# Two output tiles of a linear unit, product by product in turn instead of one after the other

## The chip, the core and the metric

The kernel runs on one core of a Trainium2 chip. Its engines work side by side, each through its own list of instructions in order: TensorE (PE, matrix products; its weight loads, PEld, run beside the products), VectorE (DVE), ScalarE (ACT), GpSimd (POOL) and the DMA queues. TensorE writes its results to PSUM, eight banks of 512 float32 per partition; DVE and ACT read them from there into SBUF. The metric is the device time of one execution in microseconds.

## The reference

Two layers over 256 latent tokens (`x`) and 256 context tokens (`ctx`), model width 1024. Per layer:

```
m = silu(c) @ w_mod + b_mod                                  # shifts, scales, gates
xn = rmsnorm(x, norm1) * (1 + m[1]) + m[0]                   # the context likewise, with c_ctx
u = xn @ w_in                                                # queries, keys, values, gates, z of three mixers
ya = blockwise_attend(...); yb = window_attend(...); yc = gdn_out(gated_delta(...), z)
y = (sig(ga)*(ya @ w_pa) + sig(gb)*(yb @ w_pb) + sig(gc)*(yc @ w_pc)) @ w_out
x = x + m[2] * y
x = x + m[5] * conv_ffn(rmsnorm(x, norm2) * (1 + m[4]) + m[3])   # silu(a) * b, width 2816, depthwise conv
```

The output is the final RMSNorm of the latent tokens. The second layer's context stream is needed only as keys, values and state, so most of that layer's linears have 256 columns and the first layer's have 512.

## The kernel before

Activations stand feature-major: a tile is 128 features by 512 tokens (context first, then latent). Every float32 value that a linear multiplies is cut in two parts of the type float32r, a high part H and the rest L, and a product is replaced by three: H·XH, H·XL, L·XH (`mm3`, L202 to L206; the three lines L204, L205, L206 are the three products, and most rows of the profile on TensorE stand under them).

`linear` (L278) goes through the weight matrix in units of 256 output features, that is two tiles of 128 features, each with a PSUM bank of its own. The weights of a unit come in loads of 4 feature blocks (512 KB): `load_split` (L186) transfers them (`raw`, three buffers), ACT rounds them to H (`wh`, L194, three buffers) and DVE or POOL forms L (`wl`, L184, four buffers). One load holds the columns of both tiles. For each load `products` (L303) issues all twelve products of the first tile (4 blocks of 3), then all twelve of the second. After its last load a tile is evicted by `evac`, at raised priority. So the first tile of a unit is finished twelve products before the second.

```
for i in range(nt):
    due = g
    for k in range(g):
        ...
        self.mm3(pss[i][:, cs[i]], H[:, k, cc], L[:, k, cc], XH[kg + k][:, cs[i]], XL[kg + k][:, cs[i]], ...)
```

PSUM is shared out by two tags: `mm` has three banks, `g` has five (L161). Outside the merge, the output projection and the feed-forward all units take their two banks from `mm`; in those three stages (`self.wide`) units take them from `mm` and `g` by turns. Everything else on TensorE (attention, the delta rule, transposes, norms) uses `g`.

The work around the linears is written as generators: a chain (delta rule or attention) yields the time that it leaves free, and `fill` (L219) emits queued linears for that long. A linear yields after every two feature blocks of one tile (`ly` = 2, six products). The library's scheduler then fixes the order of each engine's list from the order of emission, from priorities and from its own estimates; on the chip each engine goes through its list strictly in order.

What evicts a unit: the delta rule's projections one ACT and two DVE operations (L664, L667, L669), the gates a sigmoid on ACT (L1374), plain projections a copy on ACT or DVE by turns (L540, L538), the merge a DVE product (L1538, L1540), the residuals one DVE operation (L1560), the feed-forward one ACT and two DVE operations (L1600, L1603, L1605). `gdn_misc`, `proj_sq`, `linear_first` and the latent attention's values call `mm3` or its lines directly.

Of the kernel before, what the change touches and what calls it, by code (L numbers as in the profile page):

```python
# [11 lines left out]
PSUM = bass.MemoryType.PSUM  # L12
# [4 lines left out]
T = 512  # L17
S = 256
# [11 lines left out]
def make_consts():  # L30
    """Constants that depend on shapes alone: identities, masks, rotation tables."""
# [73 lines left out]
class _Tok:  # L105
    """[:, streams, tile] of a [p, 512] view: the chunks (0, 3) or (1, 2) of each stream."""
# [9 lines left out]
class Lat(float):  # L116
    """Yielded: what comes next waits for other engines, for about so many microseconds."""


class _Pri:  # L120
    """An engine whose instructions are scheduled as if they came `off` instructions earlier."""
# [13 lines left out]
class Kernel:  # L135
# [41 lines left out]
    def split_L(self, out, x, h):  # L177
        """out = x - h, exact: h is x rounded to 12 significant bits."""
        self.lacc += self.lpool
        e = self.nc.vector  # L180
        if self.lacc >= 1.0:
            self.lacc -= 1.0
            e = self.nc.gpsimd
        e.tensor_tensor(out=out, in0=x, in1=h.bitcast(F32), op=ALU.subtract)  # L184

    def load_split(self, srcs, shape):  # L186
        """Weights to SBUF (pieces: (view of the tile, source)), split exactly in two float32r parts."""
# [31 lines left out]
    def fill(self, us, burst=0.0):  # L219
        """Emit queued independent work worth about us microseconds of the tensor engine."""  # L220
# [17 lines left out]
    def bg_steps(self):  # L238
        """Steps of a later modulation while the second stream's norm is on its way."""
# [7 lines left out]
    def gate_step(self):  # L247
        """A step of the gates that are computed ahead; its time."""
# [11 lines left out]
    def ahead(self, credit=None):  # L260
        """Let the gates fill the wait of what comes next."""
# [5 lines left out]
    def gsync(self):  # L267
        """Complete the gates' unit in progress."""
        while self.gates is not None and self.gate_n[0] > self.gate_n[1]:
            self.gate_step()  # L270

    def finish(self, *gens):
        """Emit what is left of the queued gens."""
# [5 lines left out]
    def linear(self, w, k0, nk, c0, ncol, X, evac, cols=None, kgrp=4, split=None, hook=None, gate=False):  # L279
        """Feature-major product: evac(i, psum, cols) gets rows i*128.. of w[k0*128:, c0:c0+ncol].T @ X  # L280
        (c0 a tuple: the first columns of two tiles).
        The unit of columns `split` takes one stream after the other; the generator hook() advances within the
        second (or within the first, if the unit is the first)."""
        XH, XL = X
        for u0 in range(0, ncol, 256):
# [17 lines left out]
            def products(kg, wt, cs):  # L303
                """The products of one load, and each tile's evacuation after its last; yields per tile."""
                g, H, L = wt
                for i in range(nt):
                    due = g
                    for k in range(g):
                        cc = slice(i * 128, i * 128 + 128)
                        self.mm3(pss[i][:, cs[i]], H[:, k, cc], L[:, k, cc], XH[kg + k][:, cs[i]], XL[kg + k][:, cs[i]],  # L310
                                 kg + k == 0, kg + k == nk - 1)
                        if hk:
# [3 lines left out]
                        elif k % self.P["ly"] == self.P["ly"] - 1 and k < g - 1:  # L316
                            yield (cs[i].stop - cs[i].start) * self.P["ly"] * 3 / 2400
                            due -= self.P["ly"]
                    if kg + g == nk:
                        with self.tc.high_priority(self.P["hpe"]):  # L320
                            evac(u0 // 128 + i, pss[i], cs[i])
                    yield (cs[i].stop - cs[i].start) * due * 3 / 2400
# [18 lines left out]
    def rstd(self, out, ss, scale, shape, post=1.0):  # L341
        """out = post / sqrt(ss * scale + eps); for more than a few values a first guess from the bits, then Newton steps
        to float32's accuracy."""
# [15 lines left out]
    def stat(self, x, cs, first, e=None, alloc=True, last=False):  # L359
        """Add the squares of x to the running sums of columns cs; the last ones are added by stat_rstd's products."""  # L360
# [13 lines left out]
    def stat_rstd(self, cs, dim, wait=1.5):  # L374
        """Broadcast (in PSUM) 1/rms of the columns from the running sums; yields between its products."""
# [18 lines left out]
    def norm_mod(self, x, A, B, XH, XL, s, r=None, ks=range(KD)):  # L394
        """XH + XL = x * rstd * A + B for the columns of stream s."""
# [56 lines left out]
    def modulation_first(self):  # L452
        """Parts 0 and 1 of layer 0's modulation, the first half of the features before the second."""
# [26 lines left out]
    def first_norm(self, hf):  # L480
        """The features of one half, normed and modulated, of layer 0's input."""
# [7 lines left out]
    def linear_first(self, w, c0, X, evac):  # L489
        """As linear, 512 columns: the products of the first half of the features, while the modulation of the second is on its way."""  # L490
# [23 lines left out]
    def load_x(self):  # L514
# [3 lines left out]
        # x, ctx: token-major loads, transposed on PE  # L518
# [23 lines left out]
    def load_vectors(self, l):  # L542
        """The layer's vectors, one row per 128 values, transposed; yields between loads and transposes (of those first needed, and the rest)."""
# [21 lines left out]
    def load_conv(self, l):  # L565
        """The feed-forward's convolution weights, transposed."""
# [15 lines left out]
    def modulation(self, l, cg, room="raw"):  # L582
        """Parts 2cg and 2cg+1 of the modulation of layer l."""
# [25 lines left out]
    def mod_A(self, l, j, ks=slice(0, KD)):  # L609
        """A = norm * (1 + scale); j = 0 for norm1, 1 for norm2."""  # L610
# [1113 lines left out]
```

## Time and profile before

| | |
|---|---|
| three timed runs | 1824.82, 1826.38, 1837.09 us; median 1826.38 |
| span of the profiled execution (first to last instruction) | 1830.3 us; its own device time is not listed apart |
| TensorE busy | 1712.1 us (94%), 12343 instructions |
| weight loads busy | 1364.8 us, 12343 instructions |
| DVE, ACT, POOL busy | 1083.0, 773.8, 569.8 us |
| mean granted TensorE clock | 0.966 of full speed |

One execution was profiled. Each instruction has a start and a duration; products are pipelined, so the durations of neighbours overlap and the pace is read from their starts. "Idle before" with an arrow names what ended an engine's wait. The windows view gives busy time per engine in stretches of the span, with the mean granted clock of TensorE (1.00 is 2.4 GHz, 0.50 is 1.2 GHz).

### The profile page before, as it was taken

How to read it: one execution, taken by the hardware profiler on the slowest of the kernel's cores; microseconds unless marked ns; L12 is line 12 of the kernel's file. 1: busy time of each engine (PE TensorE's matmuls, PEld its weight loads, DVE VectorE, ACT ScalarE, POOL GpSimd, SP SyncE). 2: the span in 40 equal slices, each digit the busy share in tenths (PEclk: the TensorE clock that was granted, in tenths of full speed). 3: DMA queues.
4: the chain of work that ended last, by engine and by line, in shares of the span. 5: the costliest groups of instructions: out<-in, count | busy, mean ns of one | idle time of the engine just before them, and what ended most of it. 6: DMA issues, size and time to landing. Idle time of an engine off the chain costs nothing. (4 is left out here: it accounts for less than half of the span.)

```text
span 1830.3 us, 30777 instructions
## 1 busy us (share of the span) xinstructions
PE 1712.1 (94%) x12343; PEld 1364.8 (75%) x12343; DVE 1083.0 (59%) x2041; ACT 773.8 (42%) x1375; POOL 569.8 (31%) x405
## 2 busy tenths in 40 slices
PE   8899978999999999999999999889888899989997
PEld 4667764776557888558888888768777767989997
DVE  3778384464865443435425544688687776667574
ACT  3474311233756233324324333455513376555453
POOL 2152621332210423012212222152833331534242
PEclk9899989999999999999999999989988899989999
DMA  8423316233134543753332344323433223745653
GB/s 306 130 69 104 94 47 208 71 75 110 52 118 147 187 130 112 265 172 115 95 101 92 93 154 150 93 76 105 110 82 69 59 81 102 227 136 173 187 172 129
DMA packets 216941, 228.70 MB, mean 125 GB/s; under 512 B 51228, under 2 KB 195422, under 8 KB 215646
## 3 DMA queue, kind: packets, MB, share of 16 engines
q1 hardware_dynamic: 211582, 220.11, 39.6%
q10 hardware_dynamic: 4928, 6.56, 1.0%
q8 instruction: 97, 1.59, 0.4%
q14 instruction: 46, 0.38, 0.1%
q0 software_dynamic: 288, 0.06, 0.0%
HBM read 213.85 MB, written 11.80 MB: 123 GB/s over the span
## 5 line engine op out<-in xcount | busy, mean ns | idle before, releaser
L184 POOL TENSOR_TENSOR wl<-raw,wh 128x1024 fp32r<-128x1024 f32 (+3 forms) x124 | 285.2, 2301 | 700.5 <-ACT wh L194 643.1
L194 ACT CAST wh<-raw 128x1024 fp32r<-128x1024 f32 (+2 forms) x294 | 297.9, 1017 | 433.2 <-PE mm L205 195.9
L204 PE MATMUL mm<-xnh,wh 128*128 128x512 f32 (+2 forms) x1072 | 386.1, 361 | 7.5 <-DVE b L669 5.2
L206 PE MATMUL mm<-xnh,wl 128*128 128x512 f32 (+2 forms) x1072 | 379.7, 355 | 10.9 <-POOL wl L184 7.1
L205 PE MATMUL mm<-xnl,wh 128*128 128x512 f32 (+2 forms) x1072 | 380.1, 355 | 2.8 <-DVE xnl L411 2.8
L184 DVE TENSOR_TENSOR wl<-raw,wh 128x1024 fp32r<-128x1024 f32 (+1 forms) x170 | 211.1, 1243 | 197.4 <-ACT wh L194 184.6
L206 PEld LDWEIGHTS mm<-xnh,wl 128*128 128x128 f32 (+1 forms) x1072 | 209.2, 195 | 45.6 <-POOL wl L184 10.0
L204 PEld LDWEIGHTS mm<-xnh,wh 128*128 128x128 f32 (+1 forms) x1072 | 209.9, 196 | 44.4 <-issue 10.3
L205 PEld LDWEIGHTS mm<-xnl,wh 128*128 128x128 f32 (+1 forms) x1072 | 209.9, 196 | 34.8 <-issue 6.2
L204 PE MATMUL g<-xnh,wh 128*128 128x256 f32 (+1 forms) x496 | 167.1, 339 | 1.4 <-ACT xnh L410 1.4
L205 PE MATMUL g<-xnl,wh 128*128 128x256 f32 (+1 forms) x496 | 166.5, 337 | 1.8 <-DVE xnl L411 1.8
L206 PE MATMUL g<-xnh,wl 128*128 128x256 f32 (+1 forms) x496 | 166.4, 337 | 0.0
L205 PE MATMUL mm<-s,wh 128*128 128x256 f32 (+1 forms) x458 | 150.2, 329 | 2.4 <-DVE s L1204 1.3
L204 PE MATMUL mm<-s,wh 128*128 128x256 f32 (+1 forms) x458 | 151.1, 331 | 1.0 <-DVE s L538 0.5
L206 PE MATMUL mm<-s,wl 128*128 128x256 f32 (+1 forms) x458 | 150.2, 330 | 0.0
L204 PEld LDWEIGHTS g<-xnh,wh 128*128 128x128 f32 x496 | 94.3, 191 | 18.8 <-issue 6.7
L1621 POOL TENSOR_TENSOR b<-b,b 128x512 f32<-128x512 f32 (+1 forms) x44 | 53.8, 1223 | 163.5 <-DVE b L1605 156.4
L205 PEld LDWEIGHTS g<-xnl,wh 128*128 128x128 f32 x496 | 94.5, 191 | 13.4 <-DVE xnl L411 2.5
L206 PEld LDWEIGHTS g<-xnh,wl 128*128 128x128 f32 x496 | 94.5, 191 | 12.2 <-issue 2.5
L205 PE MATMUL g<-s,wh 128*128 128x512 f32 (+1 forms) x304 | 102.4, 337 | 0.9 <-DVE s L200 0.9
L204 PE MATMUL g<-s,wh 128*128 128x512 f32 (+1 forms) x304 | 102.8, 338 | 0.4 <-ACT s L199 0.4
L206 PE MATMUL g<-s,wl 128*128 128x512 f32 (+1 forms) x304 | 102.4, 337 | 0.0
(289 smaller groups left out, 2926.1 us busy)
## 6 DMA issues: line engine op xcount, KB each, us to landing
raw<-in_w_in_dram SPq DMA_DIRECT2D x92, 512.0 KB
raw<-in_ffn_up_dram SPq DMA_DIRECT2D x80, 512.0 KB
s<-in_w_mod_dram SPq DMA_DIRECT2D x64, 512.0 KB
raw<-in_w_mod_dram SPq DMA_DIRECT2D x32, 512.0 KB
raw<-in_ffn_down_dram SPq DMA_DIRECT2D x32, 512.0 KB
raw<-in_w_out_dram SPq DMA_DIRECT2D x16, 512.0 KB
raw<-in_ffn_down_dram SPq DMA_DIRECT2D x16, 384.0 KB
spill<-s SPq DMA_DIRECT2D x4, 1024.0 KB
```

The lines of the kernel that those rows point to most:

```text
L184: e.tensor_tensor(out=out, in0=x, in1=h.bitcast(F32), op=ALU.subtract)
L194: nc.scalar.copy(H, raw)
L204: mm(ps, lhsT=wH, rhs=xH, start=start, stop=False)
L205: mm(ps, lhsT=wH, rhs=xL, start=False, stop=False)
L206: mm(ps, lhsT=wL, rhs=xH, start=False, stop=stop)
L1621: nc.gpsimd.tensor_tensor(out=y[:, cs], in0=y[:, cs], in1=av[t][:, cs], op=ALU.mult)
```

## The change

Within `products` the loop over the two tiles moves from the outside to the inside. For each feature block the three products are issued kind by kind, and within a kind first for one tile and then for the other: H·XH into bank 0, H·XH into bank 1, H·XL into bank 0, H·XL into bank 1, L·XH into bank 0, L·XH into bank 1. The moving operand of two neighbours is the same, the bank and the weight block change with every product. Number, size and operands of the products stay as they are, and so does their order within a bank. A yield stands now after each feature block of both tiles (six products, as before). Both tiles end together and are evicted one behind the other after the last product. The steps of a norm that advance within products (`hk`) are counted after both tiles of a block. Comments are taken out elsewhere, so that lines move up or down by a few: all products of `linear` stand under one line now.

```
-                for i in range(nt):
-                    due = g
-                    for k in range(g):
-                        cc = slice(i * 128, i * 128 + 128)
-                        self.mm3(pss[i][:, cs[i]], H[:, k, cc], L[:, k, cc], XH[kg + k][:, cs[i]], XL[kg + k][:, cs[i]],
-                                 kg + k == 0, kg + k == nk - 1)
-                        if hk:
+                mm = self.nc.tensor.matmul
+                due = g
+                for k in range(g):
+                    h, t0, t1 = kg + k, kg + k == 0, kg + k == nk - 1
+                    cc = [slice(i * 128, i * 128 + 128) for i in range(nt)]
+
+                    for a, b, first, final in ((H, XH, t0, False), (H, XL, False, False), (L, XH, False, t1)):
+                        for i in range(nt):
+                            mm(pss[i][:, cs[i]], lhsT=a[:, k, cc[i]], rhs=b[h][:, cs[i]], start=first, stop=final)
+                    if hk:
+                        for _ in range(nt):
                             hk["n"] += 1
                             if hk["n"] in self.P["hk"]:
                                 next(hk["g"])
-                        elif k % self.P["ly"] == self.P["ly"] - 1 and k < g - 1:
-                            yield (cs[i].stop - cs[i].start) * self.P["ly"] * 3 / 2400
-                            due -= self.P["ly"]
-                    if kg + g == nk:
+                    elif k < g - 1:
+                        yield (cs[0].stop - cs[0].start) * nt * 3 / 2400
+                        due -= 1
+                if kg + g == nk:
+                    for i in range(nt):
                         with self.tc.high_priority(self.P["hpe"]):
                             evac(u0 // 128 + i, pss[i], cs[i])
-                    yield (cs[i].stop - cs[i].start) * due * 3 / 2400
+                yield (cs[0].stop - cs[0].start) * nt * due * 3 / 2400
```

Counted in the two programs: `linear` issues 6498 products, 3174 of 512 columns and 3324 of 256; 5809 pairs of neighbours among them change the bank now, against 611 neighbouring pairs of these lines before.

Place A, TensorE's list, second layer, the delta rule's projections: the unit of tiles mm_10042 and mm_10043 ends and the gate unit of mm_10137 and mm_10138 begins. mm_10138 takes the bank that mm_10042 had. Before:

```order
L734 MATMUL g_9889<-cst,misc_9872 128x32 x4
L204 MATMUL mm_10043<-xnh_9329,wh_10097 128x256
L205 MATMUL mm_10043<-xnl_9330,wh_10097 128x256
L206 MATMUL mm_10043<-xnh_9329,wl_10098 128x256
L204 MATMUL mm_10043<-xnh_9329,wh_10097 128x256
L205 MATMUL mm_10043<-xnl_9330,wh_10097 128x256
L206 MATMUL mm_10043<-xnh_9329,wl_10098 128x256
L204 MATMUL mm_10137<-xnh_9329,wh_10141 128x256
L205 MATMUL mm_10137<-xnl_9330,wh_10141 128x256
```

Now:

```order
L314 MATMUL mm_10043<-xnh_9332,wl_10098 128x256
L314 MATMUL mm_10137<-xnh_9332,wh_10141 128x256
L314 MATMUL mm_10138<-xnh_9332,wh_10141 128x256
L314 MATMUL mm_10137<-xnl_9333,wh_10141 128x256
L314 MATMUL mm_10138<-xnl_9333,wh_10141 128x256
L314 MATMUL mm_10137<-xnh_9332,wl_10142 128x256
L314 MATMUL mm_10138<-xnh_9332,wl_10142 128x256
```

Before, mm_10138 comes 24 products after the first of mm_10137; now it is the second product of the unit. The two steps of the delta rule's tables that stood behind the projections (L773 and what follows) come behind all 48 products of the gate unit now, instead of behind 41 of them.

Place B, TensorE's list, second layer, plain projections: the unit of mm_10641 and mm_10642 ends and that of mm_10723 and mm_10724 begins; mm_10724 takes the bank of mm_10641 before, and of mm_10642 now. Before:

```order
L205 MATMUL mm_10642<-xnl_9330,wh_10681 128x512
L206 MATMUL mm_10642<-xnh_9329,wl_10682 128x512
L204 MATMUL mm_10723<-xnh_9329,wh_10727 128x512
L205 MATMUL mm_10723<-xnl_9330,wh_10727 128x512
L206 MATMUL mm_10723<-xnh_9329,wl_10728 128x512
```

Now:

```order
L314 MATMUL mm_10641<-xnh_9332,wl_10682 128x512
L314 MATMUL mm_10642<-xnh_9332,wl_10682 128x512
L314 MATMUL mm_10723<-xnh_9332,wh_10727 128x512
L314 MATMUL mm_10723<-xnl_9333,wh_10727 128x512
L314 MATMUL mm_10723<-xnh_9332,wl_10728 128x512
L314 MATMUL mm_10723<-xnh_9332,wh_10727 128x512
L314 MATMUL mm_10724<-xnh_9332,wh_10727 128x512
L314 MATMUL mm_10724<-xnl_9333,wh_10727 128x512
```

Before, mm_10724 starts after twelve products of mm_10723; now after four.

Place C, ACT's list, first layer, end of the latent attention and of the gates that are computed beside it (tiles mm_4890 and mm_4891 are the last gate unit; L131 rows are the attentions' work). Before:

```order
L1374 ACT_TABLE_LOAD
L1374 ACTIVATE b_1015_5356<-mm_4890 128x512
L131 ACT_TABLE_LOAD
L131 ACTIVATE sm_5307<-sm_5305,sm_4031 128x2
```

and ten rows further

```order
L1374 ACT_TABLE_LOAD
L1374 ACTIVATE b_1036_5460<-mm_4891 128x512
L131 COPY s_1028_5401<-g_5419 128x4x128
```

Now:

```order
L131 COPY s_1027_5398<-g_5399 128x4x128
L1379 ACT_TABLE_LOAD
L1379 ACTIVATE b_1035_5457<-mm_4890 128x512
L131 COPY s_1027_5398<-g_5416 128x4x128
L1379 ACTIVATE b_1036_5460<-mm_4891 128x512
```

The two sigmoids of a gate unit stand together here now, with one table load instead of three. In the whole program ACT's list has 36 table loads, against 42.

## Rows read from the trace of the kernel before

**Rows 1.** The page's span and busy time: share of the span, instructions.

```profile
span 1830.3 us, 30777 instructions
PE 1712.1 (94%) x12343; PEld 1364.8 (75%) x12343; DVE 1083.0 (59%) x2041; ACT 773.8 (42%) x1375; POOL 569.8 (31%) x405
```

**Rows 2.** Windows: stretch, length, busy time by engine (instructions), granted clock, DMA.

```profile
450.00:500.00 50.00, 47.77 (x250) 25.75 (x250) 42.92 (x123) 39.72 (x102) 14.64 (x17) 1.00 0.21 69
800.00:1120.00 320.00, 319.50 (x1414) 260.03 (x1415) 137.80 (x171) 112.52 (x150) 79.17 (x49) 1.00 0.35 109
1200.00:1250.00 50.00, 42.25 (x251) 32.69 (x251) 43.44 (x90) 27.75 (x54) 22.98 (x16) 0.90 0.26 78
```

**Rows 3.** Timeline of TensorE, 512 columns: start us, us, instruction; mm to g.

```profile
1103.24 0.39 PE L205 MATMUL mm<-s,wh 128*128 128x512 f32 x1
1103.47 0.39 PE L206 MATMUL mm<-s,wl 128*128 128x512 f32 x1
1103.69 0.39 PE L204 MATMUL g<-s,wh 128*128 128x512 f32 x1
1103.92 0.39 PE L205 MATMUL g<-s,wh 128*128 128x512 f32 x1
```

**Rows 4.** Timeline of TensorE, 256 columns, g to mm.

```profile
1704.74 0.28 PE L206 MATMUL g<-s,wl 128*128 128x256 f32 x1
1704.86 0.28 PE L204 MATMUL mm<-s,wh 128*128 128x256 f32 x1
```

**Rows 5.** Timeline of the weight loads, one beside rows 3.

```profile
1103.47 0.19 PEld L204 LDWEIGHTS g<-s,wh 128*128 128x128 f32 x1
```

**Rows 6.** Timeline of TensorE, three tiles in turn, one moving operand.

```profile
1437.49 0.51 PE L204 MATMUL mm<-s,wh 128*128 128x256 f32 x3
```

**Rows 7.** Waits of TensorE: line, waited for: us in total, times, longest.

```profile
PE mm L206 <- POOL wl L184: 7.1, 6, 1.6
PE mm L206 <- DVE wl L184: 3.8, 2, 3.6
PE mm L205 <- DVE xnl L411: 2.8, 2, 2.0
PE g L205 <- DVE xnl L411: 1.8, 2, 1.6
```

**Rows 8.** Timeline at place A: the bank's last eviction and TensorE.

```profile
1199.46 0.48 DVE L669 SCALAR_TENSOR_TENSOR b<-mm,vec,b 128x255 f32<-128x255 f32 x1
...
1196.86 0.43 PE L734 MATMUL g<-cst,misc 32*128 32x32 f32 x4
1197.22 0.39 PE L204 MATMUL mm<-xnh,wh 128*128 128x256 f32 x1
...
1204.57 0.60 PE L773 MATMUL g<-gtb,cst 128*128 128x32 f32 x4 [1.46 <-DVE gtb L755]
```

**Rows 9.** Timeline at place B: DVE, then TensorE.

```profile
1268.97 4.16 DVE L131 STREAM_TRANSPOSE s<-s 128x1024 f32<-128x1024 f32 x2
1276.85 0.68 DVE L538 COPY s<-mm 128x512 f32<-128x512 f32 x1
...
1272.57 0.39 PE L204 MATMUL mm<-xnh,wh 128*128 128x512 f32 x1
1276.21 0.50 PE L204 MATMUL mm<-xnh,wh 128*128 128x512 f32 x1 [0.76 <-ACT s L540]
```

**Rows 10.** Timeline of two gate evictions on ACT, and TensorE beside them.

```profile
1254.65 1.28 ACT L1374 ACT_TABLE_LOAD   x1
1255.94 0.66 ACT L1374 ACTIVATE b<-mm 128x256 f32<-128x256 f32 x2
...
1254.61 0.36 PE L204 MATMUL mm<-xnh,wh 128*128 128x256 f32 x1
```

**Rows 11.** Timeline of ACT at place C.

```profile
574.03 0.60 ACT L1374 ACTIVATE b<-mm 128x512 f32<-128x512 f32 x1
```

**Rows 12.** The view of the `mm` tiles: the residuals' eviction, ns min/median/max.

```profile
L1560 DVE SCALAR_TENSOR_TENSOR s<-mm,mod,s x36: 471/480/485, 703.9 to 1821.1; 128x256 f32<-128x256 f32 x36
```

More of the change, by code (lines that the diff above doesn't have):

```diff
@@ L116 @@
 class Lat(float):
+    pass
 class _Pri:
```

## The prediction

> **What bounds the kernel now.** I read the page first, then the windows, then TensorE's timeline where it is full, its waits, and the order of both programs. The page gives a span of 1830.3 us with TensorE busy 94% of it [rows 1]. DVE, the next engine, has 59%. The windows show two kinds of stretches [rows 2]: the feed-forward of the first layer, where TensorE is busy 319.50 of 320.00 us at clock 1.00, and the delta rule of the second, where it is busy 42.25 of 50 us at 0.90 while DVE has 43.44. So in the first kind only the pace of a product counts, in the second the waits. About 118 us of the span are idle on TensorE (1830.3 - 1712.1), nearly all in the second kind.
>
> **The pace: what the change touches most.** 6498 products get a new neighbour. Does a product that changes bank and weight block start sooner or later? In a full stretch products of 512 columns start 0.22 to 0.23 us apart, within a bank and across the change from mm to g alike [rows 3]; at 256 columns the step across a change is 0.12 us [rows 4]. At 2.4 GHz the columns alone take 0.213 and 0.107 us, so each product pays some 0.013 us beyond them, and it pays them within a bank as well as across. Every product has its own weight load of 0.19 us, even where the block repeats; it lies beside the product before [rows 5]. And the pattern of the change stands in the trace already: three tiles in turn, three banks, three weight blocks, one moving operand, take 0.51 us for three products, which is two steps of (0.51 - 0.28)/2 = 0.115 us [rows 6], rounded to 0.01. I take the pace as unchanged: 0 us. Bounds: at 0.115 instead of 0.12 for all 3324 products of 256 columns it would be -17 us; nothing in the rows shows a step that is longer.
>
> **What is gained.** TensorE waits for L parts eight times, 10.9 us together [rows 7]. L is needed now after four products instead of two, so each wait shrinks by at most 0.45 us (two products of 0.227) or 0.24: I take eight times 0.3, -2.4 us. The waits for a fresh norm (4.6 us [rows 7]) are for the first features, with one product more in front of them: -1.0 us. ACT loses six table loads (42 to 36 in its list) of 1.28 us [rows 10]: 7.7 us on an engine that is 42% busy [rows 1]. In the attention the exponentials wait behind them; I take a third, -2.5 us, between 0 and -7.7. Sum of gains: -5.9 us.
>
> **What is lost: the bank.** Before, the first tile's eviction lay under the second tile's twelve products, and the next unit began with one bank. Now both tiles end together and the next unit needs its second bank with its second product. Where units take mm and g by turns (merge, output projection, feed-forward) the bank has been free for a whole unit. Elsewhere there are three banks for two. Counted in the order with 0.227 and 0.120 us a product, less than 3 us of products lie between the last use of a bank and its next in 29 units, against 10 before. Against the times of the evictions in the trace, four places come out:
> - Place A: the second product of the gate unit would stand at about 1197.3 us, but the last reader of its bank, a DVE operation, ends at 1199.46 + 0.48 = 1199.94 [rows 8]: a new wait of 2.6 us. Behind it in TensorE's list stand the transposes L717 and L734, and DVE waits for L734 to make the tables that L773 takes. Before, L734 ran at 1196.86 and L773 at 1204.57, 7.7 us later. Now L734 comes after the wait and some 18 products (2.2 us): 4.8 us later, and L773 with it. Seven products more (0.8 us) are done by then. +4.0 us; bounds 1.5 (if the present wait of 1.46 us gives its part back) to 5.
> - Place B: the four products before the first on mm_10724 end at 1272.57 + 4 x 0.227 = 1273.5; the copy out of its bank stands behind 4.16 us of DVE transposes and ends at 1276.85 + 0.68 = 1277.53 [rows 9]. Wait 4.0 us, instead of 0.76 now: +3.3 us. Behind it stand the rest of the unit and, by its weight buffers, ACT's next cast.
> - A gate unit at 1254.6: its second product meets two sigmoids behind a table load, the first done at about 1256.3 [rows 10]; before, it stood twelve products (1.44 us) further on and had to wait some 0.3 us: its wait is 1.4 to 1.6 us now, +1.1 to 1.3; I take +1.1.
> - Place C: both sigmoids of the last gate unit come where the second was, which ends at 574.03 + 0.60 = 574.6 [rows 11]; by the order the merge's second tile has up to 2.1 us less of products in front of it than before. 0 to 2.1 us; +1.5.
> Together +9.9 us. Last, where a norm waits for the last unit of a residual (twice in each layer), the first tile's eviction of 0.48 us [rows 12] no longer lies under products: four times, +1.9 us.
>
> Here a rule of the Trainium skill speaks against the change: Perfetto Trace Analysis, section Matmuls, asks that independent groups rotate through the banks so that the eviction of one group lies under the products of the next. By it the change gives up one such cover in every unit; the trace agrees in kind, but the rows leave a price only at the places above.
>
> **The sum.** 0 - 5.9 + 9.9 + 1.9 = +5.9 us. On the span that is 1830.3 + 5.9 = 1836.2. The span is 3.9 us above the median of the three runs (1826.38) and inside their spread (1824.82 to 1837.09); what lies around it is not listed, so I put the sum on the median: 1832.3, say 1832.
>
> **Rivals.**
> - The banks decide (slower). If not four but all 19 additional short handovers wait, by 1.5 us each, the loss is 28 instead of 9.9 us: 1850. It decides from the point where DVE or ACT runs some microseconds behind, as in rows 8 and 9. For it: DVE is busy 43 of 50 us in that stage [rows 2]. Against it: in the other handovers the eviction is done in time by the trace. With more chains late behind them, as at place A, it goes over 1844.6, which is 1% above the median. 0.15.
> - The clock falls (slower). If alternation left gaps at every product, the granted clock would fall in the linears. At a mean of 0.90, as in the delta rule [rows 2], the 320 us alone would become 320/0.90 = 356, so 1868 and more. Against it: the attention's stretch, in which products go round the g banks, has 1.00 [rows 2], and rows 6 show no gap. 0.03. The Trainium skill (TensorE: Matmul & The Clock Gate, section on a second HAM failure mode) tells of such a case, where cycling through banks let the clock swing; no row here shows it.
> - Products in one bank wait for each other (faster). If the 0.013 us beyond the columns came from the bank that is written twice in a row, alternation would take them off: 6498 x 0.0134 = 87 us, 1739. Against it: rows 3 show the same step where the bank changes. 0.02.
> - The gains are larger (faster). If the L waits go wholly (10.9 us), the six table loads count in full (7.7) and the step is 0.115 at 256 columns (17), less the 11.8 of losses: -24, 1802. 0.04; half of it stays within 1%.
> - The change does nothing. The order shows that it moves 5809 pairs, so the mechanism is there; a sum of zero lies inside my forecast.
>
> **How the numbers follow.** My forecast is 1832, a change within 1%, which is about what a measurement of this kernel tells from none: 0.76. Low end: the sum with the bound of the pace, 1832 - 17 = 1815. High end: 1850 of the first rival and some late chains, 1853. Its own range is 1820 to 1844. Faster by over 1%: 0.02 + 0.04 = 0.06. Slower: 0.15 + 0.03 = 0.18. Outside the range I leave about 0.06 below and 0.08 above.
>
> **What would show it.** Pace: in the feed-forward, products of the new line 0.227 and 0.120 us apart, the stretch of 320 us as long as before to 1 us; a step of 0.213 or 0.107 would make me wrong by 87 us. Banks: TensorE's waits for DVE and ACT evictions (L669, L538, the sigmoid, by their new numbers) up by some 9 us, in the second layer's projections above all, and L773 later by about 5 us at place A. Gains: the waits for `wl` below 10.9 us, 36 table loads. Clock: a mean of 0.96 to 0.97. I am wrong in kind if the dense stretches change their length, wrong in size if the waits move elsewhere, for the scheduler has reordered DVE and ACT too, and small shifts there can open or close waits that I have not counted.

## The result and the profile after

The changed kernel takes 1840.01 us (median of six runs, 1837.15 to 1842.02), the kernel before in the same comparison 1827.64 (six runs, 1824.82 to 1837.09). The ratio is 1.0057, 95% interval 1.0043 to 1.0071: about 10.4 us slower (0.0057 x 1827.6; 7.9 to 13.0 by the interval; the two medians lie 12.4 us apart). Lines of the new kernel stand five higher behind `products`, and all products of `linear` stand under L314.

The page of the changed kernel, its span and its busy times, to set beside [rows 1]:

```profile
span 1835.4 us, 30814 instructions
PE 1704.2 (93%) x12343; PEld 1363.2 (74%) x12343; DVE 1079.7 (59%) x2041; ACT 760.6 (41%) x1369; POOL 571.6 (31%) x405
```

ACT has six instructions fewer (1375 to 1369), the table loads. The mean granted clock is 0.966 in both profiled executions. For the kernel before that is the low end: 86 timed runs of it, made with the experiments below, have 0.966 to 0.974 (median 0.970), the six of the changed kernel 0.961 to 0.966 (median 0.963). The profiled executions lie only 5.1 us apart, because the one of after is the quickest of its six and the one of before is not among the quick ones; so the profile shows where the time goes, and the timed runs show how much.

Is the pace the same? The windows view of the changed kernel, the stretch of [rows 2] in the feed-forward (columns as there):

```profile
800.00:1120.00 320.00, 317.94 (x1417) 258.57 (x1418) 135.41 (x170) 110.41 (x148) 73.95 (x45) 1.00 0.36 113
```

and TensorE's timeline at the place of [rows 3], 512 columns (x2 and x4: neighbours of one form stand in one row):

```profile
1102.11 0.62 PE L314 MATMUL mm<-s,wl 128*128 128x512 f32 x2
1102.57 1.07 PE L314 MATMUL mm<-s,wh 128*128 128x512 f32 x4
1103.47 0.62 PE L314 MATMUL mm<-s,wl 128*128 128x512 f32 x2
1103.93 1.07 PE L314 MATMUL mm<-s,wh 128*128 128x512 f32 x4
```

Six products from 1102.57 to 1103.93: (1103.93 - 1102.57)/6 = 0.227 us a product, as before; at 256 columns the changed kernel shows 0.120 us (30 products from 1199.73 to 1203.33 us). The stretch now holds one wait of 2.1 us for an L part (320 - 317.94), at 825.9 us, and 1417 instructions instead of 1414. From 836 to 1165 us of before, the same product starts 1.6 us later in the changed kernel at the beginning and at the end: nothing is won or lost there.

So the loss is in waits. TensorE's waits over the whole span, changed kernel (line, waited for: us in total, times, longest):

```profile
PE mm L314 <- DVE b L674: 21.9, 5, 8.2
PE mm L314 <- DVE s L543: 5.1, 1, 5.1
PE g L314 <- DVE wl L184: 2.1, 1, 2.1
PE mm L314 <- POOL wl L184: 1.7, 1, 1.7
PE mm L206 <- POOL wl L184: 0.8, 1, 0.8
PE mm L206 <- DVE wl L184: 0.4, 1, 0.4
```

and of the kernel before, the rows that answer to the first two:

```profile
PE mm L204 <- DVE b L669: 5.2, 4, 1.9
PE mm L204 <- DVE s L538: 0.5, 1, 0.5
```

L674 (L669 before) is the last of the three operations that evict a projection of the delta rule, L543 (L538 before) the copy that evicts a plain one. The waits for L parts fell from 10.9 [rows 7] to 2.1 + 1.7 + 0.8 + 0.4 = 5.0 us; the waits in the first two rows rose from 5.2 + 0.5 = 5.7 to 21.9 + 5.1 = 27.0. I also counted them bank by bank: time in which a unit's first product in a bank stands behind the bank's last reader while TensorE is free. That is 7.0 us before and 32.9 now: 2.5 at 95 us, 6.2 at 118.8, 5.1 at 150.2, 8.3 at 1240.2, 1.2 at 1253.8, 5.2 at 1282.5, 1.2 at 1427.7, and 3 us in small ones. I call this sum the handover waits below. They are not all new idle time: by the two pages TensorE idles 1835.4 - 1704.2 = 131.2 us now and 1830.3 - 1712.1 = 118.2 us before, 13.0 us more, while the handover waits grew by 25.9. Half of them stand where TensorE waited for something else before.

The timeline of the largest, changed kernel, DVE and TensorE:

```profile
1231.24 3.85 DVE L131 STREAM_TRANSPOSE s<-s 32x1024 f32<-32x1024 f32 x2
...
1236.91 1.22 DVE L184 TENSOR_TENSOR wl<-raw,wh 128x1024 fp32r<-128x1024 f32 x1
1238.05 1.40 DVE L672 SCALAR_TENSOR_TENSOR b<-mm,vec,b 128x510 f32<-128x510 f32 x2
1239.36 1.40 DVE L674 SCALAR_TENSOR_TENSOR b<-mm,vec,b 128x510 f32<-128x510 f32 x2
...
1231.69 0.39 PE L314 MATMUL mm<-xnh,wh 128*128 128x512 f32 x1
...
1240.25 0.76 PE L314 MATMUL mm<-xnh,wh 128*128 128x512 f32 x1 [8.17 <-DVE b L674]
```

The unit's first bank is free, its second one belongs to a tile whose eviction stands in DVE's list behind the transposes and sums of the scan and behind a load's L part. DVE comes to it at 1238.05; both tiles' operations stand together (x2), so the bank is free only when the first of the two L674 ends. Before, the first tile's eviction could begin twelve products (2.7 us) ahead of the second's. That alone does not make 8 us. The same transposes in the kernel before:

```profile
1223.21 3.89 DVE L131 STREAM_TRANSPOSE s<-s 32x1024 f32<-32x1024 f32 x2
```

They come 8.0 us later now (1231.24), while TensorE's products up to there are only about 1 us later. How much of this wait belongs to the common end of the two tiles, and how much to the new order of DVE's list, is not separated.

The clock is low behind these waits. Windows of the changed kernel around the three largest handovers, first the wait, then what follows it (columns as in [rows 2]; the granted clock is the third number from the end):

```profile
112.00:118.80 6.80, 0.76 (x4) 0.27 (x2) 5.68 (x8) 3.28 (x5) 6.80 (x6) 0.93 0.17 58
118.80:125.00 6.20, 6.15 (x17) 4.92 (x18) 5.83 (x4) 4.06 (x11) 4.16 (x4) 0.53 0.30 83
1232.00:1240.00 8.00, 0.08 (x1) 0.00 (x0) 7.85 (x17) 0.00 (x0) 0.00 (x0) 0.84 0.08 11
1240.00:1245.00 5.00, 4.75 (x13) 3.77 (x14) 4.62 (x14) 3.04 (x10) 0.00 (x0) 0.58 0.26 87
1277.00:1282.50 5.50, 0.49 (x3) 0.07 (x1) 5.37 (x11) 5.08 (x11) 0.57 (x1) 0.94 0.09 9
1282.50:1289.00 6.50, 6.45 (x16) 5.07 (x17) 0.00 (x0) 0.00 (x0) 1.79 (x1) 0.53 0.51 156
```

After each of these waits TensorE works at a granted clock of 0.53 to 0.58, near its lower level of 1.2 GHz; by length times missing clock that is 6.2 x 0.47 + 5.0 x 0.42 + 6.5 x 0.47 = 8.1 us (an estimate). But the clock fell in these parts before as well, for instance behind a wait for an L part (kernel before):

```profile
1228.50:1233.00 4.50, 4.50 (x11) 3.58 (x12) 3.63 (x24) 0.00 (x0) 0.00 (x0) 0.51 0.71 224
```

So the 8.1 us are not an addition. Windows over the whole of the first layer's and of the second layer's projections, kernel before, then the same work in the changed kernel:

```profile
0.00:160.00 160.00, 136.63 (x645) 95.94 (x646) 104.77 (x230) 81.17 (x156) 53.00 (x44) 0.96 0.49 158
1165.00:1290.00 125.00, 108.16 (x876) 89.67 (x875) 100.91 (x202) 61.05 (x117) 47.49 (x29) 0.93 0.34 95
```

```profile
0.00:170.50 170.50, 141.43 (x659) 100.26 (x660) 115.16 (x245) 75.47 (x151) 55.21 (x44) 0.94 0.46 148
1166.60:1301.00 134.40, 108.65 (x879) 90.16 (x878) 106.11 (x203) 61.11 (x117) 47.52 (x30) 0.94 0.33 89
```

By the same estimate the low clock took 0.04 x 160 = 6.4 and now takes 0.06 x 170.5 = 10.2 us in the first layer; in the second it took 0.07 x 125 = 8.8 and takes 0.06 x 134.4 = 8.1 us. It adds some 4 us in the first layer and nothing in the second.

Where does the whole difference arise? I compared the two traces at the moments at which TensorE has done the same share of its work. Changed minus before, by stretches of before: 0 to 145 us +10.9, to 600 -5.0, to 730 +0.7, to 836 -5.0, to 1165 0.0, to 1281 +9.6, to 1450 -2.4, to the end -3.8; together +5.0, the spans' difference. The first jump lies in the delta rule's projections of the first layer. The second has two parts. Up to 1222 us nothing changes on balance. Then the changed kernel gets some 8 us ahead, because the L waits of 1.6 and 3.6 us at 1224.15 and 1228.49 and the low clock behind them are gone, and loses this and 2.5 us more in the wait at 1240. The other 7 us arise at place B, a plain projection. The falls are gains that lie in other places.

### The profile page after: what moved, and what is told of

It is laid out like the page before. It is cut to its first block, busy times and chain, and to the rows that moved or that the text cites. A ratio compares the mean times of both kernels' runs of the same rounds, so it can differ in the third digit from the quotient of the medians.

```text
span 1835.4 us, 30814 instructions
## 1 busy us (share of the span) xinstructions
PE 1704.2 (93%) x12343; PEld 1363.2 (74%) x12343; DVE 1079.7 (59%) x2041; ACT 760.6 (41%) x1369; POOL 571.6 (31%) x405
## 5 line engine op out<-in xcount | busy, mean ns | idle before, releaser
L314 PE MATMUL mm<-xnh,wh 128*128 128x512 f32 (+1 forms) x976 | 291.8, 362 | 30.6 <-DVE b L674 21.9
L314 PE MATMUL mm<-xnl,wh 128*128 128x512 f32 (+1 forms) x976 | 281.2, 353 | 0.0
L314 PE MATMUL mm<-xnh,wl 128*128 128x512 f32 (+1 forms) x976 | 279.0, 353 | 1.7 <-POOL wl L184 1.7
L314 PEld LDWEIGHTS mm<-xnh,wh 128*128 128x128 f32 x976 | 176.6, 196 | 69.0 <-issue 29.8
L314 PEld LDWEIGHTS mm<-xnh,wl 128*128 128x128 f32 x976 | 176.6, 196 | 28.9 <-issue 4.1
L314 PEld LDWEIGHTS mm<-xnl,wh 128*128 128x128 f32 x976 | 177.4, 196 | 24.6 <-issue 2.9
L314 PE MATMUL mm<-s,wh 128*128 128x256 f32 (+1 forms) x812 | 163.4, 322 | 0.5 <-DVE s L1565 0.5
L314 PEld LDWEIGHTS mm<-s,wh 128*128 128x128 f32 x812 | 127.0, 190 | 13.1 <-DVE s L1565 1.5
L314 PE MATMUL g<-s,wh 128*128 128x512 f32 (+1 forms) x608 | 131.3, 337 | 0.1
L314 PE MATMUL g<-xnl,wh 128*128 128x256 f32 (+1 forms) x480 | 122.0, 335 | 2.6 <-DVE xnl L416 2.5
L314 PE MATMUL g<-xnh,wh 128*128 128x256 f32 (+1 forms) x480 | 122.8, 337 | 1.1 <-ACT xnh L415 1.1
L314 PE MATMUL g<-xnh,wl 128*128 128x256 f32 (+1 forms) x480 | 121.8, 335 | 2.1 <-DVE wl L184 2.1
L314 PEld LDWEIGHTS g<-s,wh 128*128 128x128 f32 x608 | 99.1, 190 | 13.6 <-issue 1.5
L314 PE MATMUL mm<-s,wl 128*128 128x256 f32 (+1 forms) x406 | 98.7, 322 | 0.0
L314 PEld LDWEIGHTS g<-xnh,wh 128*128 128x128 f32 x480 | 82.4, 192 | 15.7 <-issue 5.0
L314 PEld LDWEIGHTS g<-xnl,wh 128*128 128x128 f32 x480 | 82.6, 192 | 12.2 <-DVE xnl L416 3.4
L314 PEld LDWEIGHTS g<-xnh,wl 128*128 128x128 f32 x480 | 82.7, 192 | 12.1 <-DVE wl L184 2.5
L1054 PE MATMUL g<-s,s 96*128 96x512 f32 (+3 forms) x192 | 83.3, 495 | 1.3 <-issue 1.3
```

What stands on the lines that cost most here:

```text
L314: mm(pss[i][:, cs[i]], lhsT=a[:, k, cc[i]], rhs=b[h][:, cs[i]], start=first, stop=final)
L1054: nc.tensor.matmul(p[:, :nk], lhsT=a[:, self.q(q0, q0 + 128)], rhs=b[:, :nk], start=j == 0, stop=j == len(ops) - 1 and not (mask and st == 1))
```

## Experiments

All edits are made in `products` unless said otherwise; "the old loop" is the loop of before, tile by tile. Each ratio is to the kernel before on the same chip (medians there 1830.05, 1829.13 and 1828.68 us).

### Which linears pay: two parts

"..." under an added condition is the old loop. The merge, the output projection and the feed-forward (`self.wide`) hold 4626 of the 6498 products, and their units take `mm` and `g` by turns; the other units hold 1872 (counted under the new line in the two traces; the 3400 and 3100 of the expectations are miscounted). First the turns outside these stages alone, then inside them alone.

```diff
+                if self.wide:
...
+                    return
```

This is narrow_only; wide_only has `if not self.wide:` there.

> The two tiles take turns only in the units that draw both banks from mm (outside the merge, the output projection and the feed-forward); the other units go tile by tile as before. Theory (the bank: both tiles end together and the next unit needs its second bank with its second product): the whole loss is here, ratio to before 1.004 to 1.008, and TensorE's waits for evictions (L674, L543 and the like) stand near 25 to 30 us as with the whole change. Rival (the pace: alternating banks or weight blocks makes a product slower by a little): 3100 of 6498 products alternate, so about half of the loss, 1.002 to 1.004, and no eviction waits beyond half.

> The turns only in the merge, the output projection and the feed-forward, where units take mm and g by turns. Theory (the bank): a bank has been free for a whole unit there, so nothing is lost: ratio 0.998 to 1.002, steps of 0.227 and 0.120 us between products. Rival (the pace): half of the loss or more, 1.003 to 1.006, with longer steps in the feed-forward.

narrow_only: 1841.64 us, ratio 1.0067 (1.0055 to 1.0079), handover waits 30.4 us. wide_only: 1825.99 us, 0.9985 (0.9974 to 0.9995), 7.6 us. So 4626 products in turns cost nothing, which ends every theory on the pace of a product, and the loss lies in the 1872 products whose units share three banks. By their number alone they would make 1872/6498 of 0.57%, a ratio of 1.0016. I ran the second kernel once more:

> The kernel of wide_only once more (turns only in the wide phase: 3400 of the 6498 products), to tell its 0.9985 from a chance. If the turns pay for themselves where no delta rule stands behind them (fewer waits for the low parts of the weights): 0.997 to 0.9995 again. If it was a chance: 0.9995 to 1.001.

1823.33 us, 0.9974 (0.9961 to 0.9988). Both runs of this kernel lie clear of the kernel before, by 0.15 and 0.26%. The page of the second:

```profile
span 1820.3 us, 30815 instructions
PE 1700.7 (93%) x12343; PEld 1362.0 (75%) x12343; DVE 1072.9 (59%) x2041; ACT 770.3 (42%) x1375; POOL 570.8 (31%) x405
```

By the traces it gains some 3 us on before between 730 and 836 us (the feed-forward beside the next layer's modulation) and 5.5 us behind 1450. That is more than the timed runs give (0.26%, 4.8 us), for the profiled execution of before is not among the quick ones. narrow_only gains nothing in the first of these stretches and 2.0 us in the second. For the last feed-forward the waits show a part of it, those of TensorE in about the last 165 us, before and then in this run (L1701 is L1677, L1584 is L1560):

```profile
PE g L1677 <- DVE s L1560: 2.1, 3, 0.9
PE mm L204 <- ACT s L199: 0.4, 1, 0.4
PE g L204 <- ACT s L199: 0.4, 1, 0.4
```

```profile
PE g L1701 <- DVE s L1584: 0.9, 2, 0.5
PE mm L333 <- DVE b L1629: 0.4, 1, 0.4
```

The waits of the final transposes (L1677) for the residual and those for fresh operands (L199) shrink. Together that is 2.9 - 1.3 = 1.6 us. What makes the 3 us beside the modulation I could not tell apart.

### Which projections: the delta rule's

`gdn_part` passes `delta=True` to `linear`; every other linear takes turns, and then the reverse.

```diff
+                if delta:
...
+                    return
```

This is turns_but_delta; delta_only has `if not delta:`.

> The turns everywhere but in the delta rule's three projections (six units in each layer less those of linear_first), which go tile by tile as before. Theory (the loss is made where the evictions are long and DVE is behind: one ACT and two DVE operations for each tile): the three long waits of the changed kernel at that place (2.5, 6.2, 5.1 us in the first layer, 8.3 us in the second) go, the 5.2 us behind the copy in the second layer stays; TensorE's waits for evictions 12 to 15 us, ratio 0.998 to 1.003. Rival (any unit that draws from mm loses alike): the loss shrinks only by the share of these units, about a fifth: 1.004 to 1.007.

> The complement: the turns only in the delta rule's projections, all other units tile by tile as before. Theory: the waits at that place stay (5 to 8 us each, less where the gate unit behind begins with one tile), the one of 5.2 us behind the copy is gone; waits for evictions 15 to 25 us, ratio 1.002 to 1.006. Rival: 1.000 to 1.002.

turns_but_delta: 1834.31 us, 1.0020 (1.0005 to 1.0034), 18.8 us of handover waits. delta_only: 1842.61 us, 1.0073 (1.0059 to 1.0088), 23.1 us. The 528 products of the delta rule's projections, of 6498, are enough for a loss as large as narrow_only's (1.0067). Their eviction is long (one ACT and two DVE operations) and goes through DVE, which runs the scan there. Two expectations missed: delta_only lies above the theory's 1.006, and turns_but_delta has more waits than 12 to 15 us, 4.8 and 2.6 of them for the delta rule's evictions in the first layer, although its units take the old loop there. The effects do not add: turns in the other narrow stages cost 0.35% where the delta rule keeps the old loop (1.0020 against 0.9985, two chips) and turns everywhere else cost nothing where it takes turns too (1.0057 against 1.0073). Turns in the gates' units, which stand between, are not to blame:

> Turns in the wide phase and in the units of the gates; the delta rule's and the plain projections as before. Theory (the loss is made by the shared banks in the delta rule's own projections): about as wide_only, 0.997 to 1.001, with handover waits of 7 to 10 us. Rival (the gates' units, which stand between the projections, hand the loss on): 1.002 to 1.005.

Here the old loop is taken `if not (self.wide or gate)`. 1824.63 us, 0.9981 (0.9968 to 0.9993), as the theory said, though with 16.5 us of handover waits instead of 7 to 10. By this, what turns_but_delta loses comes from the remaining 528 products outside the wide stages, the plain projections among them (place B is one).

### Is it the bank?

`NMM` = 4 gives units outside the wide stages four banks for two, and leaves four for everything else. The same edit to the kernel before is the control.

```diff
-        self.NRAW, ..., self.NMM = ..., 3
+        self.NRAW, ..., self.NMM = ..., 4
```

> The whole change, with four banks for mm and four for g instead of three and five. Theory (the bank): two units follow each other without sharing a bank, so the waits for evictions in the linears fall from about 30 us to under 10, and the time to 1820 to 1832 unless the chains on g miss their fifth bank. Rival (the pace, or a chain that is late for another cause than the bank): stays at 1836 to 1842. The kernel before with four banks is measured apart, since the split of banks may cost or gain by itself.

> The kernel before with four banks for mm and four for g, the control for the changed kernel with four banks (1.0013). If the fifth g bank is worth something to the chains, this is slower than before: 1.001 to 1.004, and the change with four banks stands level with it (the bank theory). If it comes out at 1.000 or faster, the change keeps a loss of 0.1% or more that four banks do not cure.

With the change 1833.52 us, 1.0013 (0.9996 to 1.0029), handover waits 3.4 us. That is 1.5 us above the range of the theory and clear of the rival's. Without it 1833.76 us, 1.0029 (1.0018 to 1.0041), 0.7 us. With four banks the change costs nothing more against its own control, so the loss hangs on the shared bank. It is not the mean clock: both have a median of 0.964, about that of the changed kernel (0.963). But the fourth bank is no cure: TensorE's waits for ACT's SiLU of the same projections, in the changed kernel and then in the kernel before, both with four banks, take its place:

```profile
PE g L695 <- ACT s L678: 17.0, 5, 7.6
```

```profile
PE g L690 <- ACT s L673: 9.3, 3, 4.8
```

DVE and ACT are late with these tiles anyway; where the unit does not wait for the eviction, the transposes behind it do.

### Which end of a unit

The change has two effects at a border: both tiles end together, and the next unit's second bank is needed with its second product. Three edits soften one or the other.

The first, turns_of_three, issues three products of one tile and then three of the other:

```diff
-                    for a, b, first, final in (...):
-                        for i in range(nt):
+                    for i in range(nt):
+                        for a, b, first, final in (...):
```

last_load_in_blocks takes the old loop for the last load of a unit, first_load_in_blocks for the first (`if kg == 0:`):

```diff
+                if kg + g == nk:
...
+                    return
```

> The tiles take turns by feature block: three products into one bank, then three into the other, so that the bank changes a third as often, while both tiles still end together and the next unit needs its second bank with its fourth product. Theory (the bank): nearly the whole loss stays, 1.004 to 1.008, less only by two products (0.24 to 0.45 us) at each wait. Rival (the single change of bank or of weight block costs): the loss falls to a third, 1.001 to 1.003.

> The turns in all loads but a unit's last, which goes tile by tile, so that the first tile ends twelve products before the second and is evicted under them, while the next unit still needs both banks at once. Theory, with the late eviction as the main half: waits for evictions under 15 us, ratio 0.999 to 1.003. With the early need of the second bank as the main half: waits stay at 25 us or more, 1.003 to 1.006. By the order the second bank comes 2.7 to 4.4 us of products after its last use at these places, against 3.6 to 5.0 with the whole change, and 4.1 to 7.8 before, which speaks for the second.

> Turns as in the change, but the first load of each unit (four features) tile by tile, as before: the second tile's bank is needed twelve products into a unit and not with its second product. Theory (the new unit meets its second bank too early): handover waits fall from 33 to below 15 us, ratio 1.000 to 1.004. Rival (what counts is that both evictions come together at a unit's end, which this leaves as it is): waits of 20 us and more, 1.004 to 1.007.

turns_of_three: 1831.74 us, 1.0007 (0.9997 to 1.0018), 17.4 us of handover waits. I had expected 1.004 and more. This speaks against the theory as it was put: both tiles end together here too, the yields are those of the change, long handover waits are left (7.4 and 5.7 us), and yet no loss is clear of noise. Its rival does not gain by it, for wide_only shows no price of a product. So the common end of the tiles is not enough for the loss; which order the scheduler makes of it counts as well. last_load_in_blocks: 1836.03 us, 1.0043 (1.0029 to 1.0058), 13.3 us: the waits of its first theory with the ratio of its second, so neither holds. first_load_in_blocks: 1832.62 us, 1.0019 (1.0009 to 1.0030), with 28.5 us, where the theory wanted less than 15 and the rival a ratio above 1.004: both missed. Its waits for evictions, TensorE:

```profile
PE mm L204 <- DVE b L693: 23.2, 5, 8.1
PE mm L204 <- DVE s L562: 4.9, 3, 3.6
```

Twelve products (2.7 us at 0.227) are too few to cover evictions that are 6 to 8 us late. And the sum of handover waits does not order the runs: 28.5 us go with 1.0019, 13.3 with 1.0043, 23.1 with 1.0073. Part of this is what the wide stages give back, which delta_only and narrow_only lack. The rest, several us in either direction, I could not assign: each version gives the scheduler another order on DVE and ACT, and waits vanish and appear elsewhere. Versions with the old loop in the delta rule and the gates both, or with turns of three in the wide stages alone, weren't tried, and no run changes the order of DVE's and ACT's lists alone.

## Why the prediction was right or wrong

**Right in class and range.** 1832 was forecast, 1840.01 came, inside 1815 to 1853, and a change of 0.57% lies within the 1%. On its own base the sum said +5.9 us; +10.4 was measured.

**Pace 0: right.** Step 0.227 us, the dense stretch without a change, wide_only not slower. The rival that products in one bank wait for each other (87 us), and the clock's as it was put (gaps at every product), are gone: the granted clock of the dense stretch is 1.00 with alternating banks. The Trainium skill describes a second HAM failure mode (TensorE: Matmul & The Clock Gate), in which products that cycle through banks leave short idle moments and the clock swings; no run here shows it. At the three places shown above where the clock fell, a wait of 5 to 8 us for an eviction stood in front. The lower mean clock of the timed runs (0.963 against 0.970) does not tell the loss either: turns_of_three and first_load_in_blocks have 0.964 and 0.963 at 1.0007 and 1.0019.

**The bank, +9.9 us: right in kind, mis-sized; this is the step that failed.** Handover waits rose by 32.9 - 7.0 = 25.9 us, TensorE's idle time by 13.0. Place by place:
- Place A, "+4.0": no wait. The timeline of the changed kernel there, the last operation on mm_10042's bank (the third of the four tiles of 255 columns), the start of mm_10043, the start of the gate unit (48 products of 256 columns, counted back from 1203.57) and L778:

```profile
1193.68 0.48 DVE L674 SCALAR_TENSOR_TENSOR b<-mm,vec,b 128x255 f32<-128x255 f32 x1
...
1192.84 0.36 PE L314 MATMUL mm<-xnh,wh 128*128 128x256 f32 x1 [0.56 <-ACT b L669]
...
1195.79 0.40 PE L314 MATMUL mm<-xnh,wh 128*128 128x256 f32 x2
...
1207.62 0.60 PE L778 MATMUL g<-gtb,cst 128*128 128x32 f32 x4 [2.05 <-DVE gtb L760]
```

  I had kept the eviction at the time of before, 1199.46 [rows 8]. It now stands at 1193.68 and ends at 1194.16, since DVE's list was ordered anew, and the gate unit begins behind it with both tiles and without a wait, where I had 2.6 us. The wait of 0.56 us lies one tile earlier: mm_10043 runs alone there, behind mm_10042, and waits for the bank of a tile before. L773 (now L778) starts at 1207.62 instead of 1204.57, 3.05 us later, of which 1.6 were there at 1165 already.
- Place B, "+3.3" with a wait of 4.0: the wait is there, 5.06 us at 1282.55, and the clock behind it is low (6.5 x 0.47 = 3.1 us); 7 us of the difference arise here. The mechanism is as written: a copy out of the bank (L543) behind DVE's transposes (changed kernel, DVE and TensorE):

```profile
1274.61 4.05 DVE L131 STREAM_TRANSPOSE s<-s 128x1024 f32<-128x1024 f32 x2
...
1281.81 0.69 DVE L543 COPY s<-mm 128x512 f32<-128x512 f32 x1
...
1282.55 0.80 PE L314 MATMUL mm<-xnh,wh 128*128 128x512 f32 x1 [5.06 <-DVE s L543]
```

- The gate unit at 1254.6, "+1.1": nothing; it begins at 1257.08 with both tiles and without a wait. The 1.1 us at 1253.8 belong to the gate unit in front of it, which waits for a delta rule's eviction (L674); 0.7 us stood there before. Place C, "+1.5": less; between 530 and 600 us the changed kernel loses nothing (its offset goes from 6.5 to 5.9).
- Not in the list: 2.5, 6.2 and 5.1 us in the first layer's projections and 8.3 us at 1240. I looked for handovers with less than 3 us of products and dropped those whose eviction ended in time by the trace of before. At 1240 TensorE waited for an L part before, 3.6 us at 1228 [rows 7]; with that wait gone it came sooner to a bank that DVE did not clear sooner. I looked mainly in the second layer; but of the 118 idle us before, 160 - 136.6 = 23.4 lie in the first 160 us and only 125 - 108.2 = 16.8 in the second layer's projections, and the largest jump (+10.9) lies in the first.

The first rival, "all 19 by 1.5 us", was no better: few handovers wait, and four of them by 5 to 8 us, where DVE is behind. This is the case of which a rule of the Trainium skill speaks (Perfetto Trace Analysis, section Matmuls): independent groups should rotate through the banks so that an eviction lies under the next group's products. The runs agree in part, with +0.73% where it is given up beside a late DVE (delta_only), -0.15 to -0.26% where units take `mm` and `g` by turns; but turns_of_three gives the cover up in the same units and stands at +0.07%.

**Gains, -5.9 us: right in kind, too small.** `wl` waits fell by 5.9 (10.9 to 5.0) where I took 2.4: a wait of up to 3.6 us went wholly, not by 0.3. The six table loads are gone; what they gave can't be told apart. The largest of these gains did not last: what TensorE won at 1228 it lost in the wait at 1240. I had no gain at all beside the modulation (5.0 us).

**Norm joins, +1.9: right in kind, about +1.** At the second layer's second norm the wait of the sum's first product rose from 1.1 + 0.3 to 2.5 us (kernel before, then the changed one):

```profile
PE g L383 <- DVE b L372: 1.1, 1, 1.1
PE g L383 <- ACT b L368: 0.3, 1, 0.3
```

```profile
PE g L388 <- DVE b L377: 2.5, 1, 2.5
```

It is 2.5 in wide_again and 1.1 in narrow_only, which goes tile by tile there. The first layer's second norm has waits of 1.0 + 0.3 now and had 0.3 + 0.2; a wait of 0.8 us at the second layer's first norm is gone. In the last feed-forward the eviction did not lie under products before either, as the timelines show (kernel before, then the changed one):

```profile
1794.69 0.87 DVE L1560 SCALAR_TENSOR_TENSOR s<-g,mod,s 128x256 f32<-128x256 f32 x2
...
1795.22 0.33 PE L1677 MATMUL g<-cst,s 128*128 128x128 f32 x1 [0.91 <-DVE s L1560]
```

```profile
1808.30 0.88 DVE L1565 SCALAR_TENSOR_TENSOR s<-mm,mod,s 128x256 f32<-128x256 f32 x2
1808.83 0.33 PE L1682 MATMUL g<-cst,s 128*128 128x128 f32 x1 [0.46 <-DVE s L1565]
```

DVE took both tiles together before too (x2), so nothing was given up here; the wait even fell from 0.91 to 0.46 us.

So the sum was near the mark by luck, because two errors stood against each other: losses of about 21 us by stretches (10.9 + 0.7 + 9.6) instead of 11.8, gains of 16.2 (5.0 + 5.0 + 2.4 + 3.8) instead of 5.9. These stretches add up to the +5.0 us of the two profiled executions; in the timed runs it is +10.4, and where the rest lies no trace shows.

## What to carry to other kernels

Alternating two accumulations product by product cost TensorE nothing here, but the two tiles then end together, and the pair's banks are wanted back together: do it where the next unit has other banks, and where the evicting engine is behind, try keeping the tiles apart, or turns of three products, which lost nothing clear of noise. When pricing a new wait, take the evicting engine's lateness at that place (here 5 to 8 us), not the eviction's own time, look at the clock behind it, and ask whether TensorE only came to the wait sooner because another wait is gone. An eviction's time in the old trace is no bound if a scheduler orders that engine anew.

## What the hardware showed

After 5 to 8 us with hardly a product TensorE's granted clock was 0.53 to 0.58 for 5.0 to 6.5 us, by estimate 2.1 to 3.1 us each. It was not a new price in the second layer's projections, where the mean clock was 0.93 before and 0.94 after; in the first layer's it went from 0.96 to 0.94. And with one weight load for every product, blocks that change with each product took 0.227 us at 512 columns, the same as in the kernel before.
